# The order of high and low weight parts in the up projection of an encoder block

## Chip, cores and metric

The kernel runs on one core of one Trainium2 chip. The metric is the device time of one execution in microseconds, as the median of several runs. The core has a matrix engine (TensorE, PE), a vector engine (VectorE, DVE), a scalar engine (ScalarE, ACT), GpSimd (POOL) and a queue that issues DMA transfers (SyncE, SP).

## What is computed

One layer of an encoder block on 256 tokens of width 2048. A state-space mixer and a pooling mixer share an input and an output projection; then comes a gated feed-forward part, then a gated embedding, each between two normalisations. What the change touches is the feed-forward part's up projection, `hn @ w_up`, with 2048 rows and 2 x 5632 columns:

```python
D_MODEL = 2048
SEQ = 256
D_FF = 5632
...
def conv_glu(hn, w_up, conv_w, conv_b, w_down):
    up = hn @ w_up
    gate, val = jnp.split(up, 2, axis=-1)
    gate = dwconv_centred(gate, conv_w, conv_b)
    return (jax.nn.gelu(gate, approximate=True) * val) @ w_down
...
        hn = rmsnorm(h, ffn_norm_pre[i])
        ff = conv_glu(hn, w_ffn_up[i], ffn_conv_w[i], ffn_conv_b[i], w_ffn_down[i])
        h = h + rmsnorm(ff, ffn_norm_post[i])
```

## The kernel before

**Products in two parts.** All large products are made from float32 values that are cut into a high and a low part, both of a type that TensorE multiplies in one pass. ScalarE copies a weight piece to the high part (L149), VectorE subtracts that from the weight to get the low part (L150); both stand in `split`. The product is high times high, high times low and low times high; low times low is left out.

**The stages** follow each other in the order dtu (part of the input projection), xbc, z, wo (output projection), ple, up, dn (down), a second ple, gt (gate). The names of PE's groups in the profile are those of the accumulators: `dtu`, `xbc`, `z`, `woa`, `ple`, `ga` and `va` (the gate and the value half of up), `dna` and `dns`, `gt`.

**Up** (L772 to L791) runs over 11 column groups of 512. In each it makes two calls of `feature_pairs` for the gate (256 columns each), the convolution and the gelu on the gate, then two calls for the value. That is 44 calls. `hid` holds the products for down.

**One call** (L287) makes 256 columns of the result in feature-major form: two accumulators `acc[0]` and `acc[1]`, each of 128 features x 512. The first 256 of these 512 take high times high, the last 256 both cross products; `total` adds the halves. The activations' panel (`wox` in the profile) holds for each of the 16 k tiles the two parts side by side, so that one weight tile of 128 x 128 is multiplied by both parts in one matmul of 512 columns: this is a *high* matmul, with the weight's high part (L298). The weight's low part is multiplied by the activations' high part only, in a matmul of 256 columns: a *low* matmul (L300).

The weights of a call come in two loads of 1 MB (`raw`, L291, three pages in turn), each of 8 k tiles by 256 columns. A load is split in two pieces of 4 k tiles (`j` = 0 and 1), each with its own high and low tile; there are five high and five low buffers in turn. A piece has 8 high matmuls (4 k tiles by 2 features) and then 8 low ones. A call has four pieces, so 64 matmuls: 8 high, 8 low, four times over. The stretch of 128 matmuls that the profile shows as one piece of the chain of waits is two calls.

At the end of a call `total` (L303) has ScalarE copy one half of each accumulator and VectorE add the other. The accumulators take two PSUM buffers of six, so three calls can be under way.

**What sets the order.** Each engine works through its own list in order. A planner makes these lists before the run, from the order in which the program is traced, the dependencies, the buffers and its own estimate of durations: it lets splits of later pieces run ahead, and it can put a later call's matmuls ahead of ones that it takes to be not yet ready. At the start of up the panel `wox` is still being made (`panel_part`, L320: transposes on PE into `woxt`, L185 on ScalarE, L186 on VectorE), and the first two calls are mixed with that. `rfbp` is a small matmul that spreads the tokens' norm along the columns; its result is wanted by the multiplication after `total` (L780).

Of the kernel before, what the change touches and what calls it, by code (L numbers as in the profile page):

```python
# [16 lines left out]
P = 128  # L17
L = 256
D = 2048
NK = D // P  # L20
# [31 lines left out]
def build(nc, a, out):  # L52
# [5 lines left out]
    with tile.TileContext(nc) as tc, \  # L58
# [8 lines left out]
        def ins(r):  # L67
            return getattr(r, "ins", r)

        def page(name, dtype=F32):  # L70
            return gp.tile([P, 2048], dtype, tag="pg", bufs=13, name=name)
# [7 lines left out]
        def main(name):  # L79
            return [pm.tile([P, 512], F32, tag="main", name=f"{name}_{i}") for i in range(2)]  # L80
# [4 lines left out]
        def mm(o, lhsT, rhs, start, stop):  # L85
            nc.tensor.matmul(o, lhsT, rhs, start=start, stop=stop, skip_group_check=True)  # L86
# [17 lines left out]
        acc, acc2 = [main(f"dtu{t}") for t in range(2)], main("dtu2")  # L104
# [27 lines left out]
        low, among, four = small[:64, 592:593], small[:64, 593:597], small[:64, 597:601]  # L132
# [7 lines left out]
        def split(name, src, nel, cuts=()):  # L140

            if name in spare:
                hi, lo = spare.pop(name)
            else:
                hi = wp.tile([P, 1088], F32R, tag="whi", bufs=5, name=f"{name}h")
                lo = wp.tile([P, 1088], F32R, tag="wlo", bufs=5, name=f"{name}l")
            for c0, c1 in zip((0, *cuts), (*cuts, nel)):
                s = slice(c0, c1)
                last["act"] = ins(nc.scalar.copy(hi[:, s], src[:, s]))  # L149
                last["dve"] = ins(nc.vector.tensor_sub(lo[:, s], src[:, s], hi[:, s].bitcast(F32)))  # L150
            return hi, lo

        def raw(name, src, a_, b_):
            r = wp.tile([P, 2048], F32, tag="raw", bufs=3, name=name)
            last["dma"] = load(r[:, :a_ * b_].rearrange("p (a b) -> p a b", a=a_), src, True)
            return r
# [34 lines left out]
        def aside():  # L191

            for job in (work.pop(0) if work else ()):
                job()
# [92 lines left out]
        def feature_pairs(name, w, c0, get, acc):  # L287


            for u in range(2):  # L290
                r = raw(f"{name}r{u}", w[u * 1024:(u + 1) * 1024, c0:c0 + 256]  # L291
                        .rearrange("(k p) c -> p k c", p=P), 8, 256)
                for j in range(2):
                    wh, wl = split(f"{name}{u}_{j}", r[:, j * 1024:(j + 1) * 1024], 1024)
                    block = [(8 * u + 4 * j + kk, f, slice(kk * 256 + f * P, kk * 256 + (f + 1) * P))
                             for kk in range(4) for f in range(2)]
                    for k, f, s in block:
                        mm(acc[f], wh[:, s], get.both(k), k == 0, False)  # L298
                    for k, f, s in block:
                        mm(acc[f][:, L:], wl[:, s], get(k)[0], False, k == NK - 1)  # L300
                aside()

        def total(o, acc):  # L303
# [5 lines left out]
        def rms(name, parts, scale, n=1):  # L309

            base = EPS
            for i, q in enumerate(parts):
                m = tiny(f"{name}m{i}", n)
                nc.gpsimd.tensor_scalar(m, q, scale, base, op0=ALU.mult, op1=ALU.add)
                base = m
            r = tiny(f"{name}r", n)
            nc.gpsimd.tensor_tensor(r, m, mhalf[:, :n], op=ALU.pow)
            return r
# [71 lines left out]
        for u in range(0, NK, 2):  # L390
            r = [wp.tile([P, 2048], F32, tag="raw", bufs=3, name=f"dtur{u}") if u else r0, page(f"dtur{u + 1}")]
            for j in range(2):
                k = u + j
# [17 lines left out]
            for j in range(2):  # L411
                k = u + j
                with tc.issue_after(front[0]), tc.issue_after(front[1]):
                    wh, wl = split(f"dtu{k}", r[j][:, :1056], 1056, ((352, 704), (704,))[k] if k < 2 else ())
# [3 lines left out]
                def part(t, q):  # L418
                    xh, xl = (v[:, t * P:(t + 1) * P] for v in hn(k))
                    xx, ww = ((xh, wh), (xh, wl), (xl, wh))[q]  # L420
                    for n in range(3):
                        o = acc2[t][:, :352] if n == 2 else acc[t][n][:, :352]
                        mm(o, xx, ww[:, n * 352:(n + 1) * 352], k == 0 and q == 0, k == NK - 1 and q == 2)
# [257 lines left out]
        for t in range(2):  # L681
# [13 lines left out]
            r = rms(f"yn{t}", [ss], rz[t][:, 1:2], n=2)  # L695
# [76 lines left out]
        for s in range(DFF // 512):  # L772
            sc = mid(f"gr{s}")
            for i in range(2):
                ga = main(f"ga{s}{i}")
                feature_pairs(f"ug{s}{i}", w_up, s * 512 + i * 256, hf, ga)
                o = sc[:, i * 512:(i + 1) * 512]
                total(o, ga)
                v = o.rearrange("p (f t) -> p f t", f=2)
                nc.vector.tensor_tensor(v, v, rfb.unsqueeze(1).to_broadcast([P, 2, L]), op=ALU.mult)  # L780
            cv = conv(f"fc{s}", sc, 3, V_FCW + 4 * s, NF, V_FCB + 4 * s)
            nc.scalar.activation(cv, cv, AF.Gelu_apprx_tanh)  # L782
            nc.gpsimd.tensor_tensor(cv.rearrange("p (f t) -> p f t", f=4), cv.rearrange("p (f t) -> p f t", f=4),  # L783
                                    rfb.unsqueeze(1).to_broadcast([P, 4, L]), op=ALU.mult)
            for i in range(2):
                va = main(f"va{s}{i}")
                feature_pairs(f"uv{s}{i}", w_up, DFF + s * 512 + i * 256, hf, va)
                c0 = (s % 2) * 1024 + i * 512
                hd = hid[s // 2][:, c0:c0 + 512]
                total(hd, va)  # L790
                nc.vector.tensor_mul(hd, hd, cv[:, i * 512:(i + 1) * 512])  # L791
# [86 lines left out]
        for half in range(2):  # L878
            acc = [main(f"gt{half}{t}") for t in range(2)]
# [83 lines left out]
```

## Time and profile before

| What | us |
|---|---|
| median of 3 runs (1137.62 to 1139.45) | 1139.27 |
| the profiled execution | 1135.94 |
| its span | 1134.1 |
| up, steady part (325.63 to 794.91 of the span) | 469.28 |
| TensorE busy | 1117.6 |
| VectorE busy | 814.2 |
| ScalarE busy | 614.7 |

The page and the views of the trace belong to the profiled execution. The span goes from its first to its last instruction. A matmul's start is recorded; its end is modelled, and neighbours overlap, so that the pace of a run of matmuls is read from start to start and not from the length of one. In the chain of waits each row is a stretch of work that nothing held up: its start, its length, engine, name, line and the number of instructions. In the timeline a row is a group of instructions of one kind in sequence: start, length from the first start to the last end, engine, line, operation, output and inputs, shapes and count, and in square brackets how long the engine had been idle before it and what ended that.

### The profile page before, as it was taken

How to read it: one execution, taken by the hardware profiler on the slowest of the kernel's cores; microseconds unless marked ns; L12 is line 12 of the kernel's file. 1: busy time of each engine (PE TensorE's matmuls, PEld its weight loads, DVE VectorE, ACT ScalarE, POOL GpSimd, SP SyncE). 2: the span in 40 equal slices, each digit the busy share in tenths (PEclk: the TensorE clock that was granted, in tenths of full speed). 3: DMA queues.
4: the chain of work that ended last, by engine and by line, in shares of the span. 5: the costliest groups of instructions: out<-in, count | busy, mean ns of one | idle time of the engine just before them, and what ended most of it. 6: DMA issues, size and time to landing. Idle time of an engine off the chain costs nothing.

```text
span 1134.1 us, 15384 instructions
## 1 busy us (share of the span) xinstructions
PE 1117.6 (99%) x6049; PEld 968.8 (85%) x6049; DVE 814.2 (72%) x1067; ACT 614.7 (54%) x837; POOL 79.6 (7%) x91
## 2 busy tenths in 40 slices
PE   9999999999999999999999999999999999999996
PEld 9998888888888888888888888888888888887886
DVE  6659985654876666665756756668888998898573
ACT  6846543553774554454544545545565665667462
POOL 0201105200110000000000000000000000002001
PEclk9999999999999999999999999999999999999998
DMA  9942276556456555555555565556466656564752
GB/s 360 379 149 75 91 260 229 164 184 197 146 195 206 186 186 186 186 189 192 192 190 193 180 202 186 186 186 223 149 222 216 203 176 222 188 210 159 231 177 75
DMA packets 129592, 219.04 MB, mean 193 GB/s; under 512 B 3696, under 2 KB 96752, under 8 KB 128624
## 3 DMA queue, kind: packets, MB, share of 16 engines
q1 hardware_dynamic: 129232, 217.70, 57.5%
q8 instruction: 47, 0.77, 0.3%
q10 hardware_dynamic: 288, 0.36, 0.1%
q14 instruction: 25, 0.20, 0.0%
HBM read 215.95 MB, written 2.10 MB: 192 GB/s over the span
## 4 chain that ended last, share of the span: by engine, by line
PE 95%; DVE 2%; ACT 1%; POOL 1%; issue 1%; DMA 0%; POOLq 0%; DVEq 0%; ACTq 0%
PE va L86 22%; PE ga L86 21%; PE dna L86 17%; PE woa L86 8%; PE gt L86 7%; PE xbc L86 5%; PE dtu L86 4%; PE z L86 4%; PE dns L86 3%; PE pw L86 1%; PE ple L86 1%; PE yd L86 0%; DVE h L742 0%; PE seg L86 0%; DMA dtur<-w_in 0%
## 5 line engine op out<-in xcount | busy, mean ns | idle before, releaser
L86 PE MATMUL ga<-wox,ug_0h 128*128 128x512 f32 x352 | 89.7, 394 | 0.0
L86 PE MATMUL ga<-wox,ug_1h 128*128 128x512 f32 x352 | 88.8, 393 | 0.0
L86 PE MATMUL va<-wox,uv_0h 128*128 128x512 f32 x352 | 88.1, 392 | 0.0
L86 PE MATMUL va<-wox,uv_1h 128*128 128x512 f32 x352 | 88.1, 392 | 0.0
L86 PE MATMUL dna<-dn_0h,hs 128*128 128x512 f32 x248 | 74.8, 389 | 0.0
L86 PE MATMUL dna<-dn_1h,hs 128*128 128x512 f32 x248 | 74.6, 389 | 0.0
L86 PEld LDWEIGHTS va<-wox,uv_1h 128*128 128x128 f32 x352 | 63.3, 189 | 11.3
L86 PEld LDWEIGHTS va<-wox,uv_0h 128*128 128x128 f32 x352 | 63.3, 189 | 11.3
L86 PEld LDWEIGHTS ga<-wox,ug_0h 128*128 128x128 f32 x352 | 63.1, 189 | 11.4 <-ACT pl L753 0.3
L86 PEld LDWEIGHTS ga<-wox,ug_1h 128*128 128x128 f32 x352 | 63.2, 189 | 11.2
L783 POOL TENSOR_TENSOR fc<-fc,rfb 128x1024 f32<-128x1024 f32 x11 | 26.5, 2406 | 440.0 <-ACT fc L782 440.0
L86 PEld LDWEIGHTS dna<-dn_1h,hs 128*128 128x128 f32 x248 | 46.6, 188 | 9.7
L86 PEld LDWEIGHTS dna<-dn_0h,hs 128*128 128x128 f32 x248 | 46.4, 188 | 9.7
L86 PEld LDWEIGHTS va<-wox,uv_1l 128*128 128x128 f32 x352 | 48.0, 190 | 3.4
L86 PEld LDWEIGHTS va<-wox,uv_0l 128*128 128x128 f32 x352 | 48.0, 190 | 3.4
L86 PEld LDWEIGHTS ga<-wox,ug_1l 128*128 128x128 f32 x352 | 48.0, 190 | 3.4
L86 PEld LDWEIGHTS ga<-wox,ug_0l 128*128 128x128 f32 x352 | 48.0, 190 | 3.4
L86 PE MATMUL ga<-wox,ug_0l 128*128 128x256 f32 x352 | 49.3, 282 | 0.0
L86 PE MATMUL va<-wox,uv_0l 128*128 128x256 f32 x352 | 49.1, 282 | 0.0
L86 PE MATMUL va<-wox,uv_1l 128*128 128x256 f32 x352 | 49.1, 282 | 0.0
L86 PE MATMUL ga<-wox,ug_1l 128*128 128x256 f32 x352 | 49.1, 282 | 0.0
L86 PE MATMUL dna<-dn_0l,hs 128*128 128x512 f32 x124 | 39.7, 389 | 0.0
(1078 smaller groups left out, 2804.8 us busy)
## 6 DMA issues: line engine op xcount, KB each, us to landing
dn0r<-w_ffn_down SPq DMA_DIRECT2D x22, 1024.0 KB, 5.5
dn1r<-w_ffn_down SPq DMA_DIRECT2D x22, 1024.0 KB, 5.5
zr<-w_in SPq DMA_DIRECT2D x8, 1024.0 KB, 5.4
wo0r<-w_out SPq DMA_DIRECT2D x8, 1024.0 KB, 5.4
wo1r<-w_out SPq DMA_DIRECT2D x8, 1024.0 KB, 5.4
gt0r<-w_ple_gate SPq DMA_DIRECT2D x8, 1024.0 KB, 5.7
gt1r<-w_ple_gate SPq DMA_DIRECT2D x8, 1024.0 KB, 5.8
dtur<-w_in SPq DMA_DIRECT2D x14, 528.0 KB, 8.8
```

What stands on the lines that cost most here:

```text
L86: nc.tensor.matmul(o, lhsT, rhs, start=start, stop=stop, skip_group_check=True)
L783: nc.gpsimd.tensor_tensor(cv.rearrange("p (f t) -> p f t", f=4), cv.rearrange("p (f t) -> p f t", f=4), rfb.unsqueeze(1).to_broadcast([P, ...
```

## The change

Only the body of `feature_pairs` changes. Both pieces of a load are split first. Then all 16 high matmuls of the load are issued and after them all 16 low ones; in the call's second load the low ones come first and the high ones after them. A call is so 16 high, 16 low, 16 low, 16 high, and since the next call begins with high matmuls, 32 of each kind stand together from there on. The flag that ended the accumulation with the last low matmul (`k == NK - 1`) is gone, and no matmul carries it now; the flag that starts it stays with the high matmuls of k tile 0, which are still the first.

```diff
         def feature_pairs(name, w, c0, get, acc):
 
 
+            def high(u, tiles):
+                for j, (wh, _) in enumerate(tiles):
+                    for k, f, s in block(u, j):
+                        mm(acc[f], wh[:, s], get.both(k), k == 0, False)
+
+            def low(u, tiles):
+                for j, (_, wl) in enumerate(tiles):
+                    for k, f, s in block(u, j):
+                        mm(acc[f][:, L:], wl[:, s], get(k)[0], False, False)
+
+            def block(u, j):
+                return [(8 * u + 4 * j + kk, f, slice(kk * 256 + f * P, kk * 256 + (f + 1) * P))
+                        for kk in range(4) for f in range(2)]
+
             for u in range(2):
                 r = raw(f"{name}r{u}", w[u * 1024:(u + 1) * 1024, c0:c0 + 256]
                         .rearrange("(k p) c -> p k c", p=P), 8, 256)
-                for j in range(2):
-                    wh, wl = split(f"{name}{u}_{j}", r[:, j * 1024:(j + 1) * 1024], 1024)
-                    block = [(8 * u + 4 * j + kk, f, slice(kk * 256 + f * P, kk * 256 + (f + 1) * P))
-                             for kk in range(4) for f in range(2)]
-                    for k, f, s in block:
-                        mm(acc[f], wh[:, s], get.both(k), k == 0, False)
-                    for k, f, s in block:
-                        mm(acc[f][:, L:], wl[:, s], get(k)[0], False, k == NK - 1)
+                tiles = [split(f"{name}{u}_{j}", r[:, j * 1024:(j + 1) * 1024], 1024) for j in range(2)]
+                for part in ((low, high) if u else (high, low)):
+                    part(u, tiles)
                 aside()
```

## The prediction

> **What bounds the kernel now.** I read the page's busy shares and slices first, then the chain of waits, then the stage that the diff touches.
>
> ```profile
> span 1134.1 us, 15384 instructions
> ...
> PE 1117.6 (99%) x6049; PEld 968.8 (85%) x6049; DVE 814.2 (72%) x1067; ACT 614.7 (54%) x837; POOL 79.6 (7%) x91
> ...
> PE 95%; DVE 2%; ACT 1%; POOL 1%; issue 1%; DMA 0%; POOLq 0%; DVEq 0%; ACTq 0%
> PE va L86 22%; PE ga L86 21%; PE dna L86 17%; PE woa L86 8%; PE gt L86 7%; PE xbc L86 5%; PE dtu L86 4%; PE z L86 4%; PE dns L86 3%; PE pw L86 1%; PE ple L86 1%; PE yd L86 0%; DVE h L742 0%; PE seg L86 0%; DMA dtur<-w_in 0%
> ```
>
> TensorE sets the end: 95% of the chain is its matmuls, and the two groups of up (`ga`, `va`) are 43% of it. So this is a change to the one engine that matters, and what counts is how closely its matmuls follow each other. The chain in order of time (start, length, what) gives that pace for every stage:
>
> ```profile
> 52.43 11.52 PE xbc L86 x96
> ...
> 148.06 21.79 PE z L86 x96
> ...
> 227.19 65.30 PE woa L86 x288
> ...
> 325.63 22.35 PE va L86 x128
> 347.98 22.35 PE ga L86 x128
> ...
> 772.57 22.35 PE va L86 x128
> 794.91 10.91 PE dna L86 x48
> ...
> 810.58 10.88 PE dna L86 x48
> ```
>
> From 325.63 to 794.91 up is 21 stretches of 128 matmuls, all of 22.35 us (469.28 / 21 = 22.347), with no other piece between them: no wait for weights, DMA or the vector engines shows. A stretch is two calls of feature_pairs; a call has 32 high matmuls (512 columns) and 32 low ones (256 columns). How the two kinds alternate inside shows the timeline of PE within one call (start, length of the group, count):
>
> ```profile
> 501.45 2.00 PE L86 MATMUL ga<-wox,ug_1h 128*128 128x512 f32 x8
> 503.29 1.11 PE L86 MATMUL ga<-wox,ug_1l 128*128 128x256 f32 x8
> 504.25 2.00 PE L86 MATMUL va<-wox,uv_0h 128*128 128x512 f32 x8
> ```
>
> From start to start eight high take 1.84 us and eight low 0.96.
>
> **The change part by part.**
>
> *The number of matmuls, columns, loads, splits and DMAs is unchanged*; only the order of the 64 matmuls in a call is new: 16 high, 32 low, 16 high, and since the next call begins with high, runs of 32 of each. What that can remove is what a change of kind costs. In long runs of one kind the profile has both paces: 512 columns at 65.30 / 288 = 0.2267 us (wo; 10.88 / 48 in down is the same), 256 columns at 11.52 / 96 = 0.1200 (xbc, whose matmuls are all 256 wide). At these paces a stretch is 64 x 0.2267 + 64 x 0.1200 = 22.19 us; it takes 22.347. The 0.16 us left over belongs to the 8 times that a stretch goes from high to low and back, so **one such pair of changes costs 0.020 us**.
>
> Where it arises can be seen behind two other places. Down's first 48 matmuls, which follow up's last low run, take 10.91 where the same number later takes 10.88; and in the timeline of PE the first matmuls of z, behind xbc, start slowly:
>
> ```profile
> 147.77 0.28 PE L86 MATMUL xbc<-hnh,xb_1l 128*128 128x256 f32 x1
> 147.89 0.63 PE L86 MATMUL z<-z_0h,hnh 128*128 128x512 f32 x2
> 148.36 0.62 PE L86 MATMUL z<-z_0l,hnh 128*128 128x512 f32 x2
> 148.82 0.62 PE L86 MATMUL z<-z_0h,hnl 128*128 128x512 f32 x2
> 149.28 0.61 PE L86 MATMUL z<-z_0h,hnh 128*128 128x512 f32 x2
> 149.73 0.62 PE L86 MATMUL z<-z_0l,hnh 128*128 128x512 f32 x2
> 150.19 0.62 PE L86 MATMUL z<-z_0h,hnl 128*128 128x512 f32 x2
> 150.64 0.61 PE L86 MATMUL z<-z_1h,hnh 128*128 128x512 f32 x2
> ```
>
> The first six 512-wide ones take 149.28 - 147.89 = 1.39 us, the next six 1.36: 0.03 us lost once, at the entry into a wide run. The xbc run before it was long (11.29 us of it unbroken in the chain), so the entry costs the same behind a long run as behind the eight low ones ahead of down: run length doesn't make it dearer. Going the other way gains a little, since 0.03 at the entry nets to 0.020 for the pair.
>
> *Sum.* 44 calls with 4 pairs of changes each make 176; afterwards a call has one pair, 44 in all. Removed are 132 x 0.020 = **2.6 us** (2.5 in the 42 steady calls, 0.1 in the first two). Upper end: if only the entry counted, 132 x 0.03 = 4.0. Lower end: with the wide pace of z, whose 96 have one entry among them (21.79 / 96 = 0.2270), a stretch at the long paces is 22.21, a pair of changes 0.017 and the sum 2.3; below that it can't be cheap, as the long paces come from runs of 96 and 288, past the 32 asked for. I take 2.6, since the whole stretch holds both directions. The lost stop flag of the last low matmul and the turn at a load's border (low behind low, high behind high) add no instruction.
>
> The Trainium skill, "TensorE: Matmul & The Clock Gate", section on the back-to-back issue gap, states N/2.4 + 2.5 ns for a warm matmul, an estimate of 216 ns at 512 columns and 109 at 256. By that a stretch would be 20.8 us, the rest of 1.55 would be put down to the alternation, and the change would bring some 26 us (1.55 x 22 x 3/4). The runs of 96 and 288 above hold 0.120 and 0.227 with no alternation at all, so the rows decide for 2.6.
>
> *The splits and their buffers.* Both pieces of a load are now split ahead of its matmuls; ScalarE's copy and VectorE's subtraction run ahead of PE by the 5 buffers of each kind, so this costs nothing while they stay ahead. Timeline, rows of ACT, DVE and the load's issue:
>
> ```profile
> 500.75 1.05 ACT L149 CAST uv_1h<-uv40r 128x1024 fp32r<-128x1024 f32 x1 [1.75 <-PE ga L86]
> 501.83 1.23 DVE L150 TENSOR_TENSOR uv_1l<-uv40r,uv_1h 128x1024 fp32r<-128x1024 f32 x1 [1.58 <-ACT uv_1h L149]
> 503.09 0.37 SPq L118 DMA_DIRECT2D ug50r<-w_ffn_up  x1
> ...
> 504.49 0.64 ACT L306 COPY gr<-ga 128x256 f32<-128x256 f32 x2
> ```
>
> The copy waits for PE to free a high buffer; that buffer is the one of five pieces before. New release times, counted from a call's start with blocks of 8 x 0.2267 = 1.81 and 8 x 0.120 = 0.96: high parts of pieces 0 to 3 come free at 1.8, 3.6, 9.3, 11.1, low parts at 4.6, 5.5, 6.5, 7.5. The latest is piece 2's high at 9.3: it carries piece 3 of the next call, whose copy (1.05) and subtraction (1.23) end at 11.6, and whose low part is wanted first, at 11.1 + 6.5 = 17.6. **Cover 6 us.** Behind the waiting copy stand the total's copies (0.64 for two), which free an accumulator pair out of three, wanted two calls later; cover again. A raw page is free after its load's second subtraction (the issue at 503.09 follows the one that starts at 501.83), so loads now issue at 6.0 and 11.9 of a call in place of every 5.6, and land 5 us later by the list of DMA issues (count, size, us to landing):
>
> ```profile
> uv40r<-w_ffn_up SPq DMA_DIRECT2D x2, 1024.0 KB, 5.2
> uv41r<-w_ffn_up SPq DMA_DIRECT2D x2, 1024.0 KB, 4.9
> ```
>
> The load of 6.0 is there at 11.2, and the buffer for its copy is free at 14.7; the other has more. DVE's and ACT's work is the same, 72% and 54%.
>
> *The start of up* is where order matters otherwise, as the first call eats the normalised panel while it is being made. The timeline there:
>
> ```profile
> 309.83 1.12 PE L86 MATMUL ga<-wox,ug_0l 128*128 128x256 f32 x8
> 310.79 1.55 PE L86 MATMUL ga<-wox,ug_1h 128*128 128x512 f32 x6
> 312.18 1.07 PE L86 MATMUL ga<-wox,ug_0h 128*128 128x512 f32 x4
> 313.52 0.48 DVE L186 SCALAR_TENSOR_TENSOR wox<-woxt,vt,wox 128x256 fp32r<-128x256 f32 x1
> 313.75 0.46 PE L86 MATMUL rfbp<-ident,rfbw 128*128 128x128 f32 x2 [0.51 <-DVE rfbw L350]
> ```
>
> The last k tile is ready at 314.0. Today the last block (8 high, 8 low: 2.8 us) can wait for it; in the new order its low block comes first and 16 high follow, 1.0 + 3.6 = 4.6 us. If nothing filled in, that is 1.8 lost. Something does: the planner has put four high matmuls of the second call at 312.18, and PE's real hole there is 313.75 - 313.25 = 0.5, a wait for VectorE's row of the norm, which the change leaves alone. I take 0, with +1.8 and -0.5 as ends. At the other edge, up's last two high buffers come free 0.9 to 1.8 us later for down's splits; down starts ahead of need, so 0, with +1.8 as the end.
>
> **The sum** for the profiled execution: 1135.94 - 2.6 = 1133.3 (span 1131.5). The runs shown have a median 3.33 higher, so the forecast is 1139.27 - 2.6 = **1136.6 us**.
>
> **Rivals.**
> 1. *An edge takes most of it back* (panel or down's splits, +1.8): 1138.4. For it: the panel's last tile comes when most of two calls' other work is done. Against: the planner fills holes there already.
> 2. *Runs are not 32 long*, because the planner that mixes two calls at 312.18 mixes them in the steady part, or the turn is lost: with runs of 16, two pairs a call, 88 x 0.020 = 1.8, so 1137.5. Against: all 21 stretches are regular today.
> 3. *The start also loses its hole*: 1139.27 - 2.6 - 0.5 = 1136.2. For it: other matmuls stand around the wait; against: its cause is untouched.
> 4. *Slower: PE waits for a low part once a call.* Place: piece 3's subtraction on DVE, which goes in its planned order, behind ACT's copy that now waits for the last-but-one high block. It decides from 6.0 us of lateness, and 0.06 past that eats a call's gain (2.6 / 44). One subtraction late per call: 44 x 1.23 = 54, so 1139.27 - 2.6 + 54 = 1190.7. For it: the copies come in bunches, with 5.6 us between the second and the third; against: 28% of DVE is idle.
>
> **How the numbers follow.** Forecast 0.60, rival 1 0.16, rival 2 0.07, rival 3 0.06, rival 4 0.11. This kernel's measurement tells about 0.2%, 2.3 us, from no change, and the forecast lies just beyond it: of its 0.60 I count 0.48 as faster and 0.12 as same. Faster 0.48 + 0.06 = 0.54; same 0.12 + 0.16 + 0.07 = 0.35; slower 0.11. The range goes from the upper end's 4.0 saved (1135.3) to the edge loss (1138.4), each widened by the 1.8 between the lowest and the highest of the runs shown: 1133.5 to 1140.2. It leaves out rival 4 and a little.
>
> **What would show it.** Right: stretches of 128 matmuls in the chain of 22.23 us (22.35 - 0.12), `ga` and `va` alone in it, groups of 16 or 32 in the timeline, DVE and ACT busy as before, z and wo to the hundredth the same, down's first 48 at 10.88. Wrong: stretches still at 22.35 with runs of 32 (the pace is not set by the entries); PE waits on L150 or L149 in up (rival 4); a first call more than 1 us longer between 298 and 325 (rival 1).

## The result, and the profile after

| | before | after |
|---|---|---|
| median of 22 runs each, us | 1138.01 (1135.96 to 1141.02) | 1136.14 (1134.51 to 1138.23) |
| profiled execution, us | 1135.94 | 1134.8 |
| its span, us | 1134.1 | 1132.7 |

The ratio is 0.9983, with a 95% interval of 0.9975 to 0.9991: faster by 1.9 us, between 1.0 and 2.8. The page after, its span and busy shares:

```profile
span 1132.7 us, 15349 instructions
...
PE 1115.6 (98%) x6049; PEld 969.4 (86%) x6049; DVE 801.1 (71%) x1067; ACT 612.0 (54%) x837; POOL 79.7 (7%) x91
```

The chain of waits after, in order of time (start, length, what):

```profile
148.28 21.79 PE z L86 x96
...
227.40 63.95 PE woa L86 x282
...
316.68 10.03 PE ga L86 x59
326.71 22.23 PE va L86 x128
348.94 22.23 PE ga L86 x128
...
771.24 22.23 PE va L86 x128
793.47 10.88 PE dna L86 x48
```

All 21 stretches of 128 matmuls have gone from 22.35 to 22.23 us, and the steady part from 469.28 to 793.47 - 326.71 = 466.76: **2.52 us less**. z is the same to the hundredth, and wo's long run has the same 0.227 us a matmul (63.95 / 282 after). Down's first 48 matmuls, which now stand behind a run of high ones, take the 10.88 of all its others. The timeline of PE over a call's border shows the runs, in groups of eight because each piece has its own tile:

```profile
500.71 2.00 PE L86 MATMUL ga<-wox,ug_0h 128*128 128x512 f32 x8
502.55 1.98 PE L86 MATMUL ga<-wox,ug_1h 128*128 128x512 f32 x8
504.36 1.98 PE L86 MATMUL va<-wox,uv_0h 128*128 128x512 f32 x8
506.18 1.98 PE L86 MATMUL va<-wox,uv_1h 128*128 128x512 f32 x8
507.99 1.11 PE L86 MATMUL va<-wox,uv_0l 128*128 128x256 f32 x8
508.94 1.12 PE L86 MATMUL va<-wox,uv_1l 128*128 128x256 f32 x8
```

From start to start the first eight high of a run take 1.84 us, as before, and each eight after them 1.81 or 1.82. The low ones stay at 0.96. So it is the entry into a high run that costs, once a run.

The span fell by only 1.4 of these 2.5 us. The start of up gave 0.87 back. Before, the timeline of PE had there (the rows around the panel's transposes `woxt`, and the first matmuls of `ga` and of `va`; a window of time cuts off the last row's count, so only its start is used):

```profile
298.74 0.63 PE L86 MATMUL ga<-wox,ug_0h 128*128 128x512 f32 x2
...
301.68 1.10 PE L86 MATMUL ga<-wox,ug_0l 128*128 128x256 f32 x8
302.62 0.40 PE L86 MATMUL ga<-wox,ug_1h 128*128 128x512 f32 x1
302.86 0.60 PE L327 MATMUL woxt<-ident,h 128*128 128x128 f32 x4
...
325.47 0.86 PE L86 MATMUL va<-wox,uv_0h 128*128 128x512 f32 x3
```

After, the same view:

```profile
298.95 0.63 PE L86 MATMUL ga<-wox,ug_0h 128*128 128x512 f32 x2
...
301.90 0.61 PE L86 MATMUL ga<-wox,ug_1h 128*128 128x512 f32 x2
302.90 0.63 PE L336 MATMUL woxt<-ident,h 128*128 128x128 f32 x4 [0.39 <-DVE wox L186]
303.29 1.17 PE L86 MATMUL ga<-wox,ug_1h 128*128 128x512 f32 x4
304.82 0.63 PE L336 MATMUL woxt<-ident,h 128*128 128x128 f32 x4 [0.37 <-DVE wox L186]
305.20 0.71 PE L86 MATMUL ga<-wox,ug_1h 128*128 128x512 f32 x2
305.75 1.12 PE L86 MATMUL ga<-wox,ug_0l 128*128 128x256 f32 x8
...
326.55 0.61 PE L86 MATMUL va<-wox,uv_0h 128*128 128x512 f32 x2
```

From first `ga` to first `va` it was 26.73 us and is 27.60. Before, eight low matmuls stood between the first block of high ones and the next transposes; now the second high block stands there, and it needs k tiles of the panel that aren't made yet. PE idles 0.39 and 0.37 us behind VectorE's `wox`, and the eight low matmuls that could have filled these holes come at 305.75. What else the span lost lies ahead of up (0.21: 298.95 against 298.74) and behind it (0.04). The sum is -2.52 + 0.87 + 0.21 + 0.04 = -1.40.

### The profile page after: what moved, and what is told of

The parts are those of the page before. It is cut to its first block, busy times and chain, and to the rows that moved or that the text cites. A ratio compares the mean times of both kernels' runs of the same rounds, so it can differ in the third digit from the quotient of the medians.

```text
span 1132.7 us, 15349 instructions
## 1 busy us (share of the span) xinstructions
PE 1115.6 (98%) x6049; PEld 969.4 (86%) x6049; DVE 801.1 (71%) x1067; ACT 612.0 (54%) x837; POOL 79.7 (7%) x91
## 4 chain that ended last, share of the span: by engine, by line
PE 94%; DVE 3%; ACT 1%; POOL 1%; issue 1%; DMA 0%; POOLq 0%; DVEq 0%; ACTq 0%
PE va L86 22%; PE ga L86 21%; PE dna L86 17%; PE woa L86 8%; PE gt L86 7%; PE xbc L86 5%; PE dtu L86 4%; PE z L86 4%; PE dns L86 3%; DVE h L751 1%; PE pw L86 1%; PE yd L86 0%; PE seg L86 0%; DMA dtur<-w_in 0%; PE mx L86 0%
## 5 line engine op out<-in xcount | busy, mean ns | idle before, releaser
L86 PEld LDWEIGHTS va<-wox,uv_1h 128*128 128x128 f32 x352 | 66.1, 188 | 13.7
L86 PEld LDWEIGHTS ga<-wox,ug_1h 128*128 128x128 f32 x352 | 65.8, 188 | 13.6
L792 POOL TENSOR_TENSOR fc<-fc,rfb 128x1024 f32<-128x1024 f32 x11 | 26.7, 2426 | 439.1 <-ACT fc L791 439.1
L86 PEld LDWEIGHTS ga<-wox,ug_1l 128*128 128x128 f32 x352 | 45.7, 192 | 0.2
L384 DVE SCALAR_TENSOR_TENSOR fc<-gr,vt,fc 128x255 f32<-128x255 f32 x88 | 40.3, 481 | 7.7 <-ACT fc L378 7.0
L86 PEld LDWEIGHTS va<-wox,uv_1l 128*128 128x128 f32 x352 | 45.4, 192 | 0.0
```

What stands on the lines that cost most here:

```text
L384: nc.vector.scalar_tensor_tensor(o[:, lo:hi], i[:, lo + d:hi + d], vec(wcol + j * wstep + f), o[:, lo:hi], op0=ALU.mult, op1=ALU.add)
```

## The experiments

**Runs of 16.** Theory 1: each low-to-high entry, net of what the first low matmul gains, costs 0.020 us. The rival: what counts is the turn at the borders of loads.

```diff
-                for part in ((low, high) if u else (high, low)):
+                for part in (high, low):
```

> Each load high then low, no turn: runs of 16, two pairs of changes a call. Theory 1 (a pair of changes costs 0.020 us whatever the run's length): a stretch of two calls takes 22.187 + 4 x 0.020 = 22.27 us (before 22.35, changed kernel 22.23), the steady part of up 1.7 us less than before. Rival (the gain comes from the turn at the border of load and call, where the next weights belong to another load): 22.35 or close to it. The start of up, from the first ga matmul to the first va matmul, was 26.74 before and 27.60 in the changed kernel; with both pieces' high parts first, as here too, about 27.6 if the order of the first call sets it.

The chain's stretches:

```profile
349.21 22.27 PE ga L86 x128
```

22.27, as theory 1 has it; the turn has no effect of its own. The stretches with 8, 4 and 2 pairs of changes (22.35, 22.27, 22.23) lie on one line, although only the first has the stop flag and splits the pieces one by one: these two parts of the edit have no price that shows. From first `ga` (299.09) to first `va` (326.79) the start took 27.70, so the second high block ahead of the first low one costs here too. The ratio to before is 0.9993 (0.9982 to 1.0004): the trace's 1.7 less in up and 1.0 more at its start leave 0.7, too little for these runs to tell.

**Runs of 4 and of 1.** Is the price of a change fixed? Each piece's high and low matmuls are interleaved in groups of `n`:

```diff
-                    for k, f, s in block:
-                        mm(acc[f], wh[:, s], get.both(k), k == 0, False)
-                    for k, f, s in block:
-                        mm(acc[f][:, L:], wl[:, s], get(k)[0], False, k == NK - 1)
+                    for i in range(0, 8, n):
+                        for k, f, s in block[i:i + n]:
+                            mm(acc[f], wh[:, s], get.both(k), k == 0, False)
+                        for k, f, s in block[i:i + n]:
+                            mm(acc[f][:, L:], wl[:, s], get(k)[0], False, k == NK - 1)
```

> Each piece in two halves: 4 high, 4 low, so 16 pairs of changes a stretch in place of 8. Theory 1: 22.187 + 16 x 0.020 = 22.50 us a stretch, some 3.4 us more than before in all; if the slow entry (five matmuls) is cut off by the next low run, 22.44. Theory 2 (the entry repays what weight loads fell behind during a low run, so that short low runs cost less): 22.35 or less.

> High and low take turns one by one, 64 pairs of changes a stretch. Theory 1 (a fixed price of 0.020 us a pair): 22.187 + 64 x 0.020 = 23.45 us a stretch, so up takes 24 us more than before. Theory 2 (a single low matmul after a high one runs at 0.113 us, as the first of each low run does, and leaves nothing behind for the next high one to repay): 64 x (0.2267 + 0.1133) = 21.76 us a stretch, so 12 us less than before. Between them, at 22.2 to 22.4, the entry costs about what the first low one gains.

A stretch with runs of 4:

```profile
351.73 22.45 PE ga L86 x128
```

That is theory 1 with the entry cut off (22.44); per pair (22.45 - 22.187) / 16 = 0.016 us. The ratio is 1.0011 (1.0001 to 1.0022), 1.3 us more; the trace has 2.2 more in up's steady part. A stretch with runs of 1, in the first profile:

```profile
350.19 22.61 PE ga L86 x128
```

Neither 23.45 nor 21.76, nor between 22.2 and 22.4: 64 pairs at (22.61 - 22.187) / 64 = 0.007. The ratio, 0.9987 (0.9968 to 1.0006), excludes nothing. But the runs did not agree with this trace: their median was 1135.55, and they fell in two groups, nine at 1133.8 to 1136.0 us and three, the profiled one among them, at 1141.9 to 1143.5. So the same program was profiled twice more.

> The kernel with runs of one again, for its trace: of its 12 timed executions 9 took 1133.8 to 1136.0 us and 3 took 1141.9 to 1143.5, and the trace shown (stretches of 22.61) is one of the slow three. If up's pace is what has two values, a trace of the faster kind shows stretches of some 0.4 us less (8 us over 21 to 22 stretches), 22.2, at the pace of the long runs with no price for a change at all. If something outside up differs, stretches stay at 22.61 and another stage is 8 us shorter.

> The same once more: by the same two readings, stretches of 22.61 or 22.2 in up and all other stages as before, or 22.61 in both and another stage shorter.

The first of these took 1143.16 us and again had stretches of 22.61. The second took 1135.47 us, and its chain of waits reads:

```profile
349.24 22.19 PE ga L86 x128
```

Up's pace itself has two values. In this execution it is that of the long runs (22.187), with no price for 64 changes of kind. Which of the two comes holds through all 21 stretches, and it was not found what decides. Runs of 1 are no safe alternative for that reason.

**Where does the price come from?** At the pace of the wide ones 256 columns would take 0.113 us (256 x 0.2267 / 512), but they follow each other every 0.120. A guess was that the loading of weights sets the 0.120, that TensorE falls behind with it in a low run, and that the next high matmuls pay. Then wider low matmuls would end it. They add columns that don't belong there (288 and 384 wide), or low times low (512).

```diff
-                        mm(acc[f][:, L:], wl[:, s], get(k)[0], False, k == NK - 1)
+                        mm(acc[f][:, L - 128:], wl[:, s], get.both(k)[:, :L + 128], False, k == NK - 1)
```

This is the one with 384; the others have 32 in place of 128, and `acc[f]` with `get.both(k)` for 512.

> The order of before, but each low matmul is 288 columns wide in place of 256 and adds 32 columns that don't belong there, so the result changes; VectorE, ScalarE and the transfers keep their work. By 512 columns at 0.2267 us a low matmul of 288 takes 0.1275, more than the 0.120 at which 256-wide ones follow each other. Theory 1 (the price is that of a change of width): runs of eight high keep their slow entry, 1.84 us for eight, and a stretch takes 8 x (1.841 + 1.020) = 22.89. Theory 2 (in a low run TensorE falls behind with weight loads, and the next high ones pay): with low matmuls that are longer than a load nothing is left to pay, eight high take 1.813 and a stretch 8 x (1.813 + 1.020) = 22.67.

> The order of before, each low matmul 384 columns wide (128 that don't belong there are added, which changes the result), at the pace of 512-wide ones 0.170 us each. Theory 1 (a change of width costs): eight high keep about 1.84 us and a stretch takes 8 x (1.841 + 1.360) = 25.61. Theory 2 (only low matmuls shorter than a weight load leave something to pay): eight high 1.813, stretch 8 x (1.813 + 1.360) = 25.39. The run with 288 columns gave neither (eight high 1.85, eight low 1.05, unsteady); if 384 is unsteady as well, what is shown stays with the run lengths.

> The order of before, each low matmul over both parts of the activations, 512 columns (low times low is added to the product). All matmuls of up have one width, but the pieces' high and low tiles and the splits change places as before. Both theories: 128 x 0.2267 = 29.02 us a stretch, no slow entry; if the border of tiles costs something of its own (a rival to both), 29.02 + 8 x 0.020 = 29.18.

The chain with 288:

```profile
351.88 23.23 PE ga L86 x128
```

That is neither 22.89 nor 22.67: a pair of changes costs (23.23 - 22.67) / 8 = 0.070 us here.

With 384, the chain and the timeline of PE:

```profile
355.35 26.13 PE ga L86 x128
```

```profile
505.46 2.01 PE L86 MATMUL va<-wox,uv_0h 128*128 128x512 f32 x8
507.31 1.58 PE L86 MATMUL va<-wox,uv_0l 128*128 128x384 f32 x8
508.73 0.63 PE L86 MATMUL va<-wox,uv_1h 128*128 128x512 f32 x2
```

And with 512:

```profile
361.73 29.01 PE ga L86 x128
```

With one width there is no price at all: 29.01 against 128 x 0.2267 = 29.02, so borders of tiles, pieces and loads are free. With 384 the low matmuls follow each other more slowly than the 0.120, yet eight high still take 1.85 and eight low 1.42 in place of 1.36: a pair of changes costs (26.13 - 25.39) / 8 = 0.093 us. By the guess longer low matmuls leave less to pay; from 256 over 288 to 384 the price rose from 0.020 over 0.070 to 0.093. So the guess falls in this form, and theory 1 stands in a looser one: a change of width costs in most of these runs, how much depends on the widths and the run's length, and in one execution with runs of 1 it cost nothing. The run with 512 also makes the low matmuls write the whole accumulator, so the width and the columns written aren't told apart. What in TensorE causes it stays open.

**The start of up.** The new order everywhere but in the first call, then in all but the first call's first load, or its second load:

```diff
-                for part in ((low, high) if u else (high, low)):
-                    part(u, tiles)
+                if name == "ug00":
+                    for j in range(2):
+                        high(u, tiles, j)
+                        low(u, tiles, j)
+                else:
+                    for part in ((low, high) if u else (high, low)):
+                        part(u, tiles)
```

The other two have `and u == 0` or `and u == 1` in the condition. In all three `high` and `low` also take the piece as an argument (not shown).

> Only the first call of up has the old order (8 high, 8 low, four times), all others the new one. If the first call's order is what lengthened the start by 0.87 us, the first ga to the first va take 26.7 to 26.8 us, the stretches stay at 22.23 and the time is 0.9 us below the changed kernel's (0.9975 of before). If the second call's order or the splits that now come in pairs did it, the start stays at 27.6.

> In the first call of up the first load has the old order (8 high, 8 low, twice), its second load and all other calls the new one. If the loss at the start comes from k tiles 4 to 7, whose high matmuls now wait for the panel with no low block ahead of them to fill in, the first ga to the first va take 26.7 to 26.9 us. If it comes from the last k tiles (16 high after the panel is done), they take 27.5 or more. Stretches 22.23.

> The other half: in the first call of up the second load has the old order, the first load and all other calls the new one. By the k tiles 4 to 7 the start stays at 27.5 to 27.7 us with two waits of about 0.4 us for the panel in it; by the last k tiles it returns to 26.7. Stretches 22.23.

The timeline of PE with the whole first call old:

```profile
299.13 0.61 PE L86 MATMUL ga<-wox,ug_0h 128*128 128x512 f32 x2
...
302.09 1.12 PE L86 MATMUL ga<-wox,ug_0l 128*128 128x256 f32 x8
303.04 0.40 PE L86 MATMUL ga<-wox,ug_1h 128*128 128x512 f32 x1
303.28 0.60 PE L343 MATMUL woxt<-ident,h 128*128 128x128 f32 x4
...
325.92 1.52 PE L86 MATMUL va<-wox,uv_0h 128*128 128x512 f32 x6
```

The low block is back ahead of the transposes, and the start takes 26.79. With the first load alone it takes 26.99, just above the 26.7 to 26.9 that were expected:

```profile
298.97 0.61 PE L86 MATMUL ga<-wox,ug_0h 128*128 128x512 f32 x2
...
325.96 1.52 PE L86 MATMUL va<-wox,uv_0h 128*128 128x512 f32 x6
```

With the second load alone it stays at 326.78 - 299.12 = 27.66, and the waits of PE keep their two holes:

```profile
PE woxt L343 <- DVE wox L186: 0.7, 2, 0.4
```

So the first load's order accounts for 0.61 of the 0.81 that the whole call brings; the other 0.20 takes both loads. The whole call's version took 1133.8 us, a ratio to before of **0.9958** (0.9943 to 0.9974), against 0.9983 (0.9975 to 0.9991) for the changed kernel. It was not run beside the changed kernel; by the traces it has the same steady part and a start shorter by 0.81. In up its trace has 2.46 us less than before (2.52 in the steady part, 0.06 back at the start); it reaches up 0.39 later, so that its span is 2.1 shorter. The ratio stands for 4.8; the last section shows where the difference is from. The single loads came to 0.9970 (0.9958 to 0.9982) and 0.9972 (0.9962 to 0.9983), which the times don't tell apart; there the traces decide.

## Why the prediction was right

*The price of a change of kind*, 0.020 us from the stretch against the paces of the long runs, held: 22.23 was forecast for a stretch and 22.23 came, 2.5 us in the steady calls and 2.52 came. Runs of 16 fell on the same line, runs of 4 just below it (0.016 a pair). That the entry costs the same behind a run of 32 as behind one of 8 was read off z and down, and is shown by the first eight of 32 at 1.84. The price is only as general as that: with runs of 1 it was 0.007 or nothing, and with other widths 0.070 and 0.093.

*The splits and buffers* cost nothing, as forecast: no wait of PE on L149 or L150 in up. Rival 4, a wait once a call, did not come. ScalarE does wait for PE and VectorE longer than before for ScalarE's copy in some places (ACT and DVE timeline after):

```profile
513.86 1.05 ACT L149 CAST uv_1h<-uv41r 128x1024 fp32r<-128x1024 f32 x1 [1.82 <-PE va L86]
514.95 1.22 DVE L150 TENSOR_TENSOR uv_1l<-uv41r,uv_1h 128x1024 fp32r<-128x1024 f32 x1 [2.92 <-ACT uv_1h L149]
```

but nothing of that reached PE, as the 6 us of cover let expect. "DVE busy as before" did not hold: VectorE's busy time fell by 13.1 us, 9.1 of it in up's subtractions (213.28 before, 204.20 after, from 326 to 793). Before, ten of these ran while GpSimd did its multiplication (L783) and took 2.0 to 2.6 us in place of 1.22 (timeline before, POOL and DVE); after, one did.

```profile
466.83 2.41 POOL L783 TENSOR_TENSOR fc<-fc,rfb 128x1024 f32<-128x1024 f32 x1 [42.35 <-ACT fc L782]
468.26 2.06 DVE L150 TENSOR_TENSOR uv_1l<-uv31r,uv_1h 128x1024 fp32r<-128x1024 f32 x1 [1.52 <-ACT uv_1h L149]
```

That gave nothing back to the span, as PE didn't wait for VectorE there in either kernel.

*The start of up* is the term that was mis-sized: 0 was taken, within -0.5 and +1.8, and it was +0.87. The place was right (the first call meets a panel in the making), the mechanism was not. The prediction looked at the last k tile and the work left behind it. The loss came at k tiles 4 to 7, where the low block, ready and needed as filler, now stood behind a high block that had to wait. "The planner fills holes there already" failed here: it put the second high block and the transposes ahead of the ready low block. Undoing the order in the first load alone brought back most of it. This is rival 1 at half its size, together with the forecast's own gain: 2.6 forecast, 1.4 in the traces, 1.9 by the runs' ratio.

*Down's edge*, feared for the late buffers, cost nothing (10.88 from its first 48 on).

The forecast lay beyond the 0.2% that this measurement was said to tell from no change; the result, 0.17%, lies just inside, though its interval excludes no change. The 0.87 us at the start is what moved it there.

That the forecast of 1136.6 us stands so near the median of 1136.14 is in part luck. It was counted from the median of three runs, 1139.27; the 22 runs have 1138.01. From that the forecast would have been 1135.4, and the 0.7 us by which the saving fell short would show.

## What to carry to other kernels

The gain of a new order on the bounding engine can be read from the profile of before, if it holds long runs of each kind: their paces against the mixed stretch give the price of mixing. A new order that is right for the steady part may be wrong for the first call, where data is still being made; there keep short blocks of ready work between those that wait, and give the first call its own order. And a kernel whose timings fall in two groups has to be profiled until both have been seen.

## What the runs showed of the hardware

Two things were not expected. One program, with high and low matmuls in turn, ran its stretches at 22.61 us in two profiled executions and at 22.19 in a third, for the whole of up each time, with a granted clock of 1.00 over up in all three.

And the scatter of all these runs, some 5 us, has a part that the trace shows: short stretches of half clock. Here is the place where down ends and gate begins, in the kernel with runs of 16 and after the change, each in two windows of 3.41 us (window, length, busy time of PE, PEld, DVE, ACT, POOL, granted clock, DMA share, GB/s):

```profile
1034.19:1037.60 3.41, 1.12 (x7) 0.80 (x6) 3.41 (x7) 1.53 (x4) 0.00 (x0) 1.00 0.00 0
1037.60:1041.01 3.41, 3.41 (x13) 3.00 (x12) 2.69 (x4) 2.29 (x6) 0.00 (x0) 0.50 0.92 274
```

```profile
1033.66:1037.07 3.41, 1.52 (x10) 1.34 (x11) 3.41 (x6) 1.08 (x4) 0.00 (x0) 1.00 0.10 16
1037.07:1040.48 3.41, 3.41 (x17) 2.55 (x16) 3.33 (x7) 3.41 (x9) 0.00 (x0) 1.00 0.90 286
```

With runs of 16 the clock is halved for 3.41 us, and the stage from gate's first matmul to the end takes 1.4 us more than after the change. The Trainium skill, "TensorE: Matmul & The Clock Gate", Part 1, has the clock halved after an idle window of about 3.4 us; the trace agrees on the length of the window, but the one ahead was not idle: it held 1.12 us of PE's work.

All 13 traces have a hole in PE's work at two places, 2.0 us long ahead of xbc's last run and 2.3 us long here. Eight of these 26 holes are followed by half clock, always for 3.41 us. In each trace every time between two recorded changes of the clock within the span is a whole number of 3.413 us (88.75 us, 26 of them, after the drop shown above). The time is so cut into fixed windows. On these, every window with 1.51 us of PE's work or less is followed by half clock, and of those with 1.52 or more only one, with 1.522 (the ends of matmuls are modelled, so the border is rough). The same hole therefore costs 1.4 to 1.5 us where nearly all of it falls into one window, and nothing where two windows share it. Which of the two comes depends on where the windows lie, and that differs between executions of one program.

The times show the steps too. Beside each time stands the execution's mean granted clock; the traces without a drop at the two places have 0.997 or 0.998, those with one 0.996, the one with two 0.994. Here are the 29 runs of the kernel before that were compared with the version with the old first call, by their clock (one run at 0.995, 1139.39, left out):

```
0.997 or 0.998   1136.04 to 1136.94   (6 runs)
0.996            1137.63 to 1138.20   (9 runs)
0.994            1138.95 to 1141.33   (13 runs)
```

The version with the old first call ran four times at 0.997 or 0.998, 1133.49 to 1133.82, and twice at 0.996, 1134.98 and 1135.44. By the medians of each group it is 2.6 and 2.7 us below the kernel before, near the 2.46 that its trace has less in up. The rest of its ratio comes from the runs of before at 0.994, the clock of two drops, which it has none of. In the same way the changed kernel's eight runs at 0.997 have a median of 1134.9, 1.4 below the 1136.3 of these runs of before, by the 1.4 of its trace, against 1.9 by the ratio.

Whether an order makes two drops rarer was not tried by a run of its own, but the traces give a reason why it can. With windows that lie fixed, it matters how far apart the two holes are. From xbc's last run to gate's first matmul it is 900.24 us before, and 1.5 more once a drop has slowed xbc: 264.2 windows, near a whole number, so that the second hole falls much as the first did. There 14 of 29 runs have a clock below 0.996. With runs of 16 it is 264.0, and 6 of 12 have it. After the change it is 263.7 and 1 of 22, with the old first call 263.5 and 0 of 6. One or two drops are as large as the whole effect of this change, which is why the traces' stages carried the argument here.
